# Hybrid HGRN2 and MoBA layer: the first pair of MoBA's keys and queries by 512-column products with both parts of x^T

## The chip, the cores and the metric

The kernel runs on one core of a Trainium2 chip, in one launch. The metric is the device time of an execution in microseconds. Before the change the median of three executions is 497.51 us (497.19 to 497.54).

## The reference

The layer reads x (256 tokens by 1024 channels, fp32) and computes

- `proj = x @ w_in`, split into HGRN2's q, f, i, g (1024 columns each), MoBA's q, k, v (1024 each) and 2048 gate logits;
- HGRN2, a gated linear recurrence with 8 heads of 128, then an RMS norm per head, multiplied by `silu(g)`;
- MoBA, which at 256 tokens and blocks of 256 is plain causal attention, 8 heads of 128, with rotary embedding on q and k:

```
t1, t2 = halves of a head
rope(t) = [t1 * cos - t2 * sin, t2 * cos + t1 * sin]
```

- both branches through their own 1024 by 1024 matrix, mixed by sigmoid gates, through `w_out`, added to `2**0.25 * x`, a layer norm;
- a SwiGLU FFN of width 2816, again with a residual and a layer norm.

## The kernel before, in words

**Two-part products.** Each fp32 operand is kept as a high part (rounded to the format that TensorE streams quickly, float32r) and a low part, the difference. A product is high times high, plus low times high, plus high times low. `split` makes the parts: a copy on ScalarE (ACT) and a subtraction on VectorE (DVE). For weights, `stage` issues the load on SP's queue (L203), the copy (L204) and the subtraction (L206), tile by tile in the order of `plan()`, three tiles ahead of their use; there are three buffers for raw tiles and four each for high and low parts.

**x^T.** `xp` is a `Pair`: for each of the 8 slices of 128 channels, the high and the low part of x^T lie side by side, 256 tokens each. `xTh` and `xTl` are views of one part; `xp.both(k)` is both parts as one operand of 512 columns.

**Two forms of a projection by features** (128 output features on the partitions, 256 tokens along the row; a pair is two such features, which here are two heads):

- `feat_pair` (narrow): one PSUM bank for the two features. For each feature and each k, three matmuls of 256 columns (L303 to L305): high weight by high x, high weight by low x, low weight by high x, all added into the same 256 columns.
- `wide_pair` (wide): one PSUM bank per feature. For each k, one matmul of 512 columns (L293: high weight by both parts of x) and one of 256 (L294: low weight by high x, added to the first half). The sum of the two halves of the bank is made afterwards, by the caller.

MoBA's keys and queries come in four pairs of heads each. `rope_pair` (L613) makes one: the pair j = 0 by `feat_pair`, with the rotary embedding read from PSUM; the others by `wide_pair`, with the halves summed into a tile of the pool `sm`, tag sg (a copy on ACT, L619, and an add on DVE, L620), from which the embedding is read. The embedding is two copies on ACT that swap the halves (L624, L625), a multiplication by cos on DVE (L626), and a multiplication by sin and an addition on POOL (L627, L628). Tag sg has two buffers. They also hold the swapped halves `rt`, and the squares `sq` of HGRN2's norm (L517).

**PSUM.** Pool `mm` has four banks (all projections), pool `aux` the other four (recurrence, heads, transpositions).

**Order.** At the start and from the last part of the mixing to the first of the FFN, and at the end, the order on PE, DVE and ACT is written out by hand (`manual_schedule`). Between these, a planner with its own cost estimates sorts the instructions of each engine before the run; on the chip each engine then works through its list in order and waits by semaphores. The priority comes from the order in the program. There HGRN2 runs as a side task (`side.step()`): around the first key and query pair stand its last products (`sc`, L503, and `o`, L514 and L515), the norm (squares L517 on ACT, sums L519 and L520 on DVE, the power on POOL L521, the product L524 on DVE), the transpositions (`ot`, L533, on PE) and their split (L536, L537). MoBA's heads (scores L632 and L633) follow as a side task after two pairs each.

The order of the projections in the program is: values for the recurrence, its gate, half of MoBA's values, gate b, key pair 0, query pair 0, key pair 1, query pair 1, the other half of the values, pairs 2 and 3, gate a.

Of the kernel before, what the change touches and what calls it, by code (L numbers as in the profile page):

```python
# [10 lines left out]
F32 = mybir.dt.float32  # L11
# [6 lines left out]
P = 128  # L18
T = 256
# [101 lines left out]
def hybrid_layer_kernel(ctx: ExitStack, tc, x, xw, vecs, bias, wts, ln1_w, ln1_b, ln2_w, ln2_b, consts, out):  # L121
    nc = tc.nc
# [6 lines left out]
    sm = pool("sm", 2)  # L129
    klp = pool("klp", 1)  # L130
    mm = pool("mm", 4, space=PSUM)
# [106 lines left out]
    def fetch(ahead=LOOKAHEAD):  # L238
        while state["next"] < len(loads) and len(ready) < 1 + ahead:
            list(stage())  # L240
        return ready.pop(0)
# [6 lines left out]
    xp = Pair("xp")  # L248
# [27 lines left out]
    def feat_pair(name, ah=None, al=None):  # L276
        ah, al = (xTh, xTl) if ah is None else (ah, al)
        wh, wl = fetch()
        ps = mm.tile([P, 2, T], F32, tag="mm", name=name)
        for f in range(2):  # L280
            feat_steps(ps[:, f, :], wh, wl, f, ah, al, range(KC))
        return ps

    def wide_pair(name, a, p, tag):


        wh, wl = fetch()
        pss = []
        for f in range(2):
            ps = p.tile([P, 2, T], F32, tag=tag, name=f"{name}{f}")  # L290
            wcol = slice(f * P, (f + 1) * P)
            for k in range(KC):
                nc.tensor.matmul(ps, wh[:, k, wcol], a.both(k), start=(k == 0), stop=False)  # L293
                nc.tensor.matmul(ps[:, 0, :], wl[:, k, wcol], a[0, k, slice(0, T)],  # L294
                                 start=False, stop=(k == KC - 1))
            pss.append(ps)
        return pss

    def feat_steps(ps, wh, wl, f, ah, al, ks, k0=0):
        wcol = slice(f * P, (f + 1) * P)  # L300
        for k in ks:
            kk = k0 + k
            nc.tensor.matmul(ps, wh[:, k, wcol], ah[:, kk, :], start=(kk == 0), stop=False)  # L303
            nc.tensor.matmul(ps, wh[:, k, wcol], al[:, kk, :], start=False, stop=False)  # L304
            nc.tensor.matmul(ps, wl[:, k, wcol], ah[:, kk, :], start=False, stop=(kk == KC - 1))  # L305
# [99 lines left out]
    for j in range(4):  # L405
        ps = feat_pair(f"hq{j}")
        sg = sm.tile([P, 2, T], F32, tag="sg", name=f"sgq{j}")
# [203 lines left out]
    ybl = slot("ybl", F32R).rearrange("p (h t) -> p h t", h=H)  # L611

    def rope_pair(nm, dst, j):  # L613
        if j == 0:
            ps = feat_pair(f"m{nm}{j}")
        else:
            ps = sm.tile([P, 2, T], F32, tag="sg", name=f"z{nm}{j}")
            for f, parts in enumerate(wide_pair(f"m{nm}{j}", xp, mm, "mm")):
                nc.scalar.copy(ps[:, f, :], parts[:, 1, :])  # L619
                nc.vector.tensor_add(ps[:, f, :], parts[:, 0, :], ps[:, f, :])  # L620
        hs = slice(2 * j, 2 * j + 2)
        bc = lambda z: z[:, None, :].to_broadcast([P, 2, T])
        tmp = sm.tile([P, 2, T], F32, tag="sg", name=f"rt{nm}{j}")
        nc.scalar.copy(tmp[0:64], ps[64:P])  # L624
        nc.scalar.copy(tmp[64:P], ps[0:64])  # L625
        nc.vector.tensor_mul(dst[:, hs, :], ps, bc(cos))  # L626
        nc.gpsimd.tensor_mul(tmp, tmp, bc(sin))  # L627
        nc.gpsimd.tensor_add(dst[:, hs, :], dst[:, hs, :], tmp)  # L628
# [44 lines left out]
    for c in range(2):  # L673
        if c == 1:
            values(1)
        for j in range(2 * c, 2 * c + 2):
            rope_pair("k", kT, j)
            side.step()
            rope_pair("q", qT, j)
            side.step()  # L680
        side.gens.append(moba_heads(4 * c, 4))
# [318 lines left out]
```

## Time and profile before

| | |
|---|---|
| median of three executions | 497.51 us (497.19 to 497.54) |
| profiled execution | 497.34 us |
| its span | 495.5 us |
| mean granted TensorE clock | 0.995 |
| busy: PE, DVE, ACT, POOL | 486.4, 396.9, 279.4, 34.0 us |
| instructions: PE, DVE, ACT, POOL | 2662, 495, 350, 33 |

Times are microseconds from the start of the span. PE is TensorE's matmul, PEld its weight load, which overlaps; DVE is VectorE, ACT is ScalarE, POOL is GpSimd, SP the engine that issues most loads. In the order of time a row has the start, the duration, the engine, the line and what is written from what; names are those of the program without buffer numbers. Matmuls are pipelined: a matmul's duration reaches into the next one's, so that what one costs in a stream is read from the distance between starts. A product of plain fp32 operands shows as two matmuls.

### The profile page before, as it was taken

The numbers are of one execution on the slowest core, as the hardware profiler recorded it, in microseconds if no ns is written. First come the engines' busy times: TensorE is split into PE (matmuls) and PEld (weight loads), VectorE is DVE, ScalarE is ACT, GpSimd is POOL, SyncE is SP. The second block draws the span as 40 slices with busy tenths as digits, with TensorE's granted clock in tenths as the row PEclk, the third lists the DMA queues.
The fourth block names the chain that finished last, engine by engine and source line by source line (L and its number), as shares of the span: only waits on it lengthen the run. The fifth ranks groups of instructions, "written<-read, shape, count | busy, mean of one in ns | idle before, by whom it ended". The sixth has DMA issues, their size and how long they took to land.

```text
span 495.5 us, 6725 instructions
## 1 busy us (share of the span) xinstructions
PE 486.4 (98%) x2662; PEld 422.0 (85%) x2662; DVE 396.9 (80%) x495; ACT 279.4 (56%) x350; POOL 34.0 (7%) x33
## 2 busy tenths in 40 slices
PE   9999999999999999999999999999999999999993
PEld 8899888888899888888888888888888888888883
DVE  4978799999868797876595778854887778899997
ACT  5796487435546676669643462444566554565510
POOL 0000000000003631240000000000000000000001
PEclk9999999999999999999999999999999999999997
DMA  8977526644542437358455446256555454355502
GB/s 310 417 259 285 169 92 248 222 161 169 171 169 89 142 126 285 112 167 306 181 176 175 165 176 242 87 187 237 175 202 219 169 177 165 128 227 221 188 1 85
DMA packets 14703, 92.65 MB, mean 187 GB/s; under 512 B 1744, under 2 KB 1744, under 8 KB 4944
## 3 DMA queue, kind: packets, MB, share of 16 engines
q1 hardware_dynamic: 13824, 89.08, 49.7%
q0 software_dynamic: 848, 3.15, 2.0%
q8 instruction: 21, 0.34, 0.3%
q14 instruction: 10, 0.08, 0.0%
HBM read 91.17 MB, written 1.05 MB: 186 GB/s over the span
## 4 chain that ended last, share of the span: by engine, by line
PE 96%; DVE 2%; DMA 1%; issue 0%; ACT 0%; DVEq 0%
PE fu L293 7%; PE fg L293 7%; PE fg L294 3%; PE fu L294 3%; PE mq L293 2%; PE mk L293 2%; PE sc L483 2%; PE wp L923 2%; PE wp L924 2%; PE wp L922 2%; PE hq L304 2%; PE hq L305 2%; PE hq L303 2%; PE hf L317 2%; PE za L339 1%; PE za L341 1%
## 5 line engine op out<-in xcount | busy, mean ns | idle before, releaser
L206 DVE TENSOR_TENSOR wl<-raw,wh 128x2048 fp32r<-128x2048 f32 (+1 forms) x72 | 164.5, 2291 | 55.1 <-ACT wh L204 54.9
L204 ACT CAST wh<-raw 128x2048 fp32r<-128x2048 f32 (+1 forms) x72 | 135.4, 1888 | 65.7 <-PE fg L293 11.5
L293 PE MATMUL fg<-x1p,wh 128*128 128x512 f32 x144 | 50.5, 394 | 0.0
L293 PE MATMUL fu<-x1p,wh 128*128 128x512 f32 x144 | 50.4, 394 | 0.0
L294 PE MATMUL fg<-x1p,wl 128*128 128x256 f32 x144 | 40.0, 278 | 0.0
L294 PE MATMUL fu<-x1p,wl 128*128 128x256 f32 x144 | 39.9, 277 | 0.0
L293 PEld LDWEIGHTS fu<-x1p,wh 128*128 128x128 f32 x144 | 27.0, 187 | 6.2
L293 PEld LDWEIGHTS fg<-x1p,wh 128*128 128x128 f32 x144 | 27.0, 187 | 6.1
L294 PEld LDWEIGHTS fg<-x1p,wl 128*128 128x128 f32 x144 | 27.1, 188 | 0.1
L294 PEld LDWEIGHTS fu<-x1p,wl 128*128 128x128 f32 x144 | 27.1, 188 | 0.0
L304 PE MATMUL hq<-xp,wh 128*128 128x256 f32 x64 | 18.1, 283 | 0.0
L305 PE MATMUL hq<-xp,wl 128*128 128x256 f32 x64 | 18.1, 283 | 0.0
L303 PE MATMUL hq<-xp,wh 128*128 128x256 f32 x64 | 18.1, 283 | 0.0
L293 PE MATMUL mk<-xp,wh 128*128 128x512 f32 x48 | 17.5, 402 | 0.0
L293 PE MATMUL mq<-xp,wh 128*128 128x512 f32 x48 | 17.2, 399 | 0.0
L485 DVE COPY_PREDICATED SD<-cst,sc 128x512 f32<-128x512 uint32 x14 | 14.9, 1071 | 1.2 <-PE sc L483 1.0
L733 PE MATMUL wp<-wh,ap 128*128 128x512 f32 (+1 forms) x40 | 14.9, 373 | 0.0
L732 PE MATMUL wp<-wl,ap 128*128 128x512 f32 (+1 forms) x40 | 14.9, 373 | 0.0
L731 PE MATMUL wp<-wh,ap 128*128 128x512 f32 (+1 forms) x40 | 14.9, 373 | 0.0
L521 POOL TENSOR_TENSOR ost<-ost,half 128x4 f32<-128x4 f32 x4 | 4.0, 1012 | 154.0 <-DVE ost L520 154.0
L294 PE MATMUL mk<-xp,wl 128*128 128x256 f32 x48 | 13.8, 288 | 0.0
L294 PE MATMUL mq<-xp,wl 128*128 128x256 f32 x48 | 13.6, 284 | 0.0
(319 smaller groups left out, 1319.7 us busy)
## 6 DMA issues: line engine op xcount, KB each, us to landing
raw<-in_wts_dram SPq DMA_DIRECT2D x76, 1024.0 KB, 4.8
xw<-in_xw_dram SPq DMA_DIRECT2D x6, 640.0 KB, 9.6
raw<-in_wts_dram SPq DMA_DIRECT2D x2, 512.0 KB, 10.6
xr<-in_x_dram POOLq DMA_DIRECT2D x1, 1024.0 KB, 5.6
wb<-in_ln_w_dram POOLq DMA_DIRECT2D x2, 512.0 KB, 5.6
wb<-in_ln_b_dram POOLq DMA_DIRECT2D x2, 512.0 KB, 7.5
out_dram<-y SPq DMA_DIRECT2D x4, 256.0 KB, 2.1
cst<-in_consts_dram SPq DMA_DIRECT2D x1, 960.0 KB, 12.2
```

What stands on the lines that cost most here:

```text
L204: nc.scalar.copy(h[:, ks, :], raw[:, ks, :])
L206: eng.tensor_sub(l[:, ks, :], raw[:, ks, :], r32(h[:, ks, :]))
L293: nc.tensor.matmul(ps, wh[:, k, wcol], a.both(k), start=(k == 0), stop=False)
L294: nc.tensor.matmul(ps[:, 0, :], wl[:, k, wcol], a[0, k, slice(0, T)], start=False, stop=(k == KC - 1))
L303: nc.tensor.matmul(ps, wh[:, k, wcol], ah[:, kk, :], start=(kk == 0), stop=False)
L304: nc.tensor.matmul(ps, wh[:, k, wcol], al[:, kk, :], start=False, stop=False)
L305: nc.tensor.matmul(ps, wl[:, k, wcol], ah[:, kk, :], start=False, stop=(kk == KC - 1))
L317: nc.tensor.matmul(ps, wh[:, kk, wcol], xp.both(k), start=False, stop=False)
L485: nc.vector.copy_predicated(later(SD, n, 4 * g, 4), m[:, None, :, :, :].to_broadcast([P, 4, nb, NT, n]), ps.rearrange("p a (b u i) -> p a ...
L731: nc.tensor.matmul(ps, lh(kk)[:, ts], wh[:, k, ns], start=(kk == first), stop=False)
L732: nc.tensor.matmul(ps, lh(kk)[:, ts], wl[:, k, ns], start=False, stop=False)
L733: nc.tensor.matmul(ps, ll(kk)[:, ts], wh[:, k, ns], start=False, stop=(kk == ktot - 1))
```

## The change

Key and query pair 0 take the form of the other three pairs. `feat_pair` is called for HGRN2's q alone then.

```diff
     def rope_pair(nm, dst, j):
-        if j == 0:
-            ps = feat_pair(f"m{nm}{j}")
-        else:
-            ps = sm.tile([P, 2, T], F32, tag="sg", name=f"z{nm}{j}")
-            for f, parts in enumerate(wide_pair(f"m{nm}{j}", xp, mm, "mm")):
-                nc.scalar.copy(ps[:, f, :], parts[:, 1, :])
-                nc.vector.tensor_add(ps[:, f, :], parts[:, 0, :], ps[:, f, :])
+        ps = sm.tile([P, 2, T], F32, tag="sg", name=f"z{nm}{j}")
+        for f, parts in enumerate(wide_pair(f"m{nm}{j}", xp, mm, "mm")):
+            nc.scalar.copy(ps[:, f, :], parts[:, 1, :])
+            nc.vector.tensor_add(ps[:, f, :], parts[:, 0, :], ps[:, f, :])
         hs = slice(2 * j, 2 * j + 2)
```

For each of the two projections this replaces 48 matmuls of 256 columns by 16 of 512 and 16 of 256, takes two banks of `mm` in place of one, adds a tile of tag sg, two copies on ACT and two adds on DVE, and lets L624 to L626 read that tile in SBUF in place of the bank. Loads, weights and their splits stay as they are.

## The prediction

> **What bounds the kernel now.** I read the page first: the busy shares, the forty slices and the chain that ended last.
>
> ```profile
> span 495.5 us, 6725 instructions
> ...
> PE 486.4 (98%) x2662; PEld 422.0 (85%) x2662; DVE 396.9 (80%) x495; ACT 279.4 (56%) x350; POOL 34.0 (7%) x33
> ...
> PEclk9999999999999999999999999999999999999997
> ...
> PE 96%; DVE 2%; DMA 1%; issue 0%; ACT 0%; DVEq 0%
> ```
>
> TensorE is busy for 98% of the span, at full granted clock up to the last of the forty slices, and the chain is 96% PE. What no other engine can hide is PE's own issue time; work on DVE, ACT or POOL counts only where it makes PE wait. Second view: busy times in the stretch where the first key and query pair runs now, and in the next pair's (columns: stretch, length, busy us and instructions of PE, PEld, DVE, ACT and POOL, granted clock, DMA share, GB/s).
>
> ```profile
> 139.60:159.10 19.50, 19.50 (x170) 19.46 (x169) 13.36 (x27) 10.94 (x15) 3.35 (x4) 1.00 0.36 133
> 159.10:171.50 12.40, 12.40 (x75) 10.89 (x75) 10.41 (x17) 7.99 (x12) 7.85 (x5) 1.00 0.32 94
> ```
>
> PE fills both. In the first stretch DVE has 19.50 - 13.36 = 6.1 us free and ACT 8.6 us. Busy PE can hide small gaps, because a matmul's end is modelled, so the third view is the order of time on PE, from which I take start-to-start distances (columns: start, duration, engine, line).
>
> ```profile
> 29.78 0.28 PE L303 MATMUL hq<-xp,wh 128*128 128x256 f32 x1
> ...
> 41.66 0.28 PE L303 MATMUL hq<-xp,wh 128*128 128x256 f32 x1
> ...
> 156.90 0.28 PE L305 MATMUL mq<-xp,wl 128*128 128x256 f32 x1
> ...
> 159.05 0.28 PE L305 MATMUL mq<-xp,wl 128*128 128x256 f32 x1
> 159.17 0.40 PE L293 MATMUL mk<-xp,wh 128*128 128x512 f32 x1
> ...
> 165.69 0.40 PE L293 MATMUL mq<-xp,wh 128*128 128x512 f32 x1
> ...
> 170.98 0.40 PE L293 MATMUL mq<-xp,wh 128*128 128x512 f32 x1
> ...
> 339.76 0.39 PE L293 MATMUL fu<-x1p,wh 128*128 128x512 f32 x1
> ...
> 344.27 0.39 PE L293 MATMUL fu<-x1p,wh 128*128 128x512 f32 x1
> ```
>
> A step over one k is three 256-column matmuls in the narrow form, one 512 and one 256 in the wide form. Narrow: 11.88 us for the 33 steps of hq is 0.360 us a step, 2.15 us for the last 6 of mq is 0.358. Wide: 5.29 us for 15 steps of the second pair's mq is 0.353, 4.51 us for 13 steps of fu is 0.347. Both stream 768 columns; the wide one only has a matmul and a weight load less.
>
> **The change, part by part.**
>
> *TensorE.* Two projections, two features, eight k: 32 steps. 96 matmuls become 64. In place, 32 x (0.358 - 0.353) = 0.16 us less; between the rows farthest apart, 32 x (0.360 - 0.347) = 0.42 us less. No row has a wide step longer than a narrow one, so there is no loss at this term. I take 0.2 us, because the hq run and the second pair's mq, the longest uninterrupted runs of this region, give 32 x (0.360 - 0.353) = 0.22 and the in-place pair a little less. [...]
>
> *The order on PE.* The planner lays the HGRN work between these matmuls and may lay it otherwise. That costs nothing by itself:
>
> ```profile
> 150.59 0.28 PE L303 MATMUL mq<-xp,wh 128*128 128x256 f32 x1
> 150.71 0.27 PE L533 MATMUL ot<-cst,on 128*128 128x128 f32 x1
> 150.74 0.36 PE L304 MATMUL mq<-xp,wh 128*128 128x256 f32 x1
> 150.94 0.28 PE L305 MATMUL mq<-xp,wl 128*128 128x256 f32 x1
> ...
> 151.18 0.27 PE L533 MATMUL ot<-cst,on 128*128 128x128 f32 x1
> ```
>
> L303 to L305 is 0.35 us with a transposition between, against 2 x 0.12 = 0.24 without: the insertion costs 0.11 us. In the chain, four transpositions one behind the other cost the same 0.11 us each:
>
> ```profile
> 165.06 0.44 PE ot L533 x4
> ```
>
> So breaking the stream costs nothing beyond the inserted work; no gain comes from fewer breaks and no loss from more.
>
> *ACT and DVE.* Four copies (L619) and four adds (L620) are new; L624 and L625 now read the sum in SBUF, L626 too.
>
> ```profile
> L619 ACT COPY zk<-mk x6: 357/370/374, 162.6 to 205.7; 128x256 f32<-128x256 f32 x6
> L620 DVE TENSOR_TENSOR zk<-mk,zk x6: 408/414/418, 165.2 to 208.5; 128x256 f32<-128x256 f32 x6
> ...
> L624 ACT COPY rtk<-mk x1: 583/583/583, 157.5 to 157.5; 64x512 f32<-64x512 f32 x1
> ...
> L626 DVE TENSOR_TENSOR kT<-mk,cst x1: 677/677/677, 160.0 to 160.0; 128x512 f32<-128x512 f32 x1
> L624 ACT COPY rtk<-zk x3: 619/619/620, 170.6 to 209.0; 64x512 f32<-64x512 f32 x3
> L626 DVE TENSOR_TENSOR kT<-zk,cst x3: 674/680/683, 171.2 to 209.2; 128x512 f32<-128x512 f32 x3
> ```
>
> ACT: 4 x 0.370 + 4 x (0.619 - 0.583) = 1.6 us. DVE: 4 x 0.414 = 1.7 us, L626 unchanged. Both fit into the 8.6 and 6.1 us that are free under PE's matmuls, so they cost nothing; with that cover gone they would cost at most their 3.3 us in a row. The new waits are those of L619, for its bank's last matmul and a buffer of sg, and of L620 behind it; queued behind them are weight splits on both engines and the norm's squares and sums. What could be late next is thus (a) weights, (b) PSUM banks, (c) the heads that read kT and qT, and the norm, which is the first rival below.
>
> (a) Weight tiles are split long ahead. This cast waited for mk's last use of its buffer, and four buffers turn round, so it holds the tile four products on, after mq, mk and mq: mv's first (mk, mq, mk and mq are one tile each):
>
> ```profile
> 149.95 1.90 ACT L204 CAST wh<-raw 128x2048 fp32r<-128x2048 f32 x1 [1.20 <-PE mk L304]
> 151.94 2.28 DVE L206 TENSOR_TENSOR wl<-raw,wh 128x2048 fp32r<-128x2048 f32 x1
> 171.33 0.40 PE L339 MATMUL mv<-wh,xp 128*128 128x512 f32 x1
> ```
>
> Its low part ends at 154.2, 17 us before PE needs it; 3.3 us more on ACT and DVE don't reach PE. The change adds no DMA and moves none past another on SP's queue; the number of weight tiles is the same.
>
> (b) The four banks of the pool mm now hold this pair's four halves, and the second pair's first product, at 159.17 in today's order, needs the first of them. Rows for mk, a square's last reading, the end of qT's first pair on POOL, and the first scores:
>
> ```profile
> L303 PE MATMUL mk<-xp,wh x16: 277/283/283, 139.7 to 149.5; 128*128 128x256 f32 x16
> ...
> 157.55 0.69 DVE L519 TENSOR_REDUCE ost<-sq 128x4 f32<-128x512 f32 x1 [0.46 <-ACT sq L517]
> ...
> L632 PE MATMUL s<-kT,qT x16: 270/272/275, 174.1 to 244.5; 128*128 128x128 f32 x16
> ...
> 165.89 1.30 POOL L628 TENSOR_TENSOR qT<-qT,rtq 128x512 f32<-128x512 f32 x1
> ```
>
> Even all of mk is done by 149.8, over 9 us ahead; copy and add take 0.8 us. The two buffers of tag sg, into which the sum goes, are shared with the squares of the norm, the last of them read until 158.2. A half that got its buffer only then would be summed at 159.0, still ahead of 159.17. I cost it at zero; otherwise a late bank costs a copy and an add, 0.8 us.
>
> (c) Scores of the first head start at 174.1; qT of the first pair is finished on POOL at 165.89 + 1.30 = 167.2. 7 us are to spare.
>
> **The sum.** Profiled execution: 497.34 us, of which 495.5 are span and 1.84 lie around it. 497.34 - 0.2 = 497.1. That execution lies 0.17 below the median of 497.51, so for a median I forecast 497.51 - 0.2 = 497.3 us.
>
> **The rivals.**
>
> *Slower: PE waits for the HGRN norm's transpositions.* Squares, sum, power on POOL, product on DVE, transposition on PE: a chain whose PE part sits between the matmuls of this pair with next to no slack, in an order fixed before the run.
>
> ```profile
> 150.89 1.13 DVE L524 SCALAR_TENSOR_TENSOR on<-o,ost,hgs 128x128 f32<-128x128 f32 x4 [1.13 <-POOL ost L521]
> ...
> 162.34 2.33 DVE L206 TENSOR_TENSOR wl<-raw,wh 128x2048 fp32r<-128x2048 f32 x1
> ...
> 158.79 1.29 POOL L627 TENSOR_TENSOR rtk<-rtk,cst 128x512 f32<-128x512 f32 x1 [1.50 <-ACT rtk L625]
> 160.25 1.01 POOL L521 TENSOR_TENSOR ost<-ost,half 128x4 f32<-128x4 f32 x1 [0.17 <-DVE ost L520]
> ...
> 162.48 3.34 POOL L627 TENSOR_TENSOR rtq<-rtq,cst 128x512 f32<-128x512 f32 x1
> ```
>
> The transposition at 151.18 starts 0.3 us after the products of its norm began. Behind a rope multiplication on POOL stood a power (160.25), and such a multiplication took 3.34 us in place of 1.29 while a weight split ran. Should the change move the pair's rope so that a held one stands before a power, the products come 3.34 - 1.29 = 2.05 us late, and PE stands with its transposition at its head, all later matmuls behind it: 497.3 + 2.05 = 499.4. It decides once the delay exceeds the planned slack. Against it: PE has no such gap today, although one rope operation was held. Of the first pair's two multiplications by sine, one was held and the other stood before a power; that both meet in the new order, with too little slack, I put at 1 in 10. [...]
>
> *Slower: the banks.* As in (b), with 0.8 us each for both projections' first halves: 497.3 + 1.6 = 498.9. For it: all four banks are now this pair's. Against: 9 us of cover. 4 in 100.
>
> *Faster.* Each wide step at fu's 0.347 gives 0.42 us: 497.1. Over 0.2% (1.0 us, what a measurement of this kernel can tell from no change) needs more than PE's streams hold, as interruptions cost nothing. 3 in 100, for something at the ends of the run that these rows don't show.
>
> **How the numbers follow.** Forecast without visible change 83 in 100, transposition wait 10, banks 4, faster 3. Slower by over 0.2% is thus 0.13 (the banks' case is only just beyond the bound, so I count part of it as same), faster 0.03, same 0.84. Low end: 497.51 - 0.42, less 0.35 for the spread of the three runs, is 496.7. High end: 497.3 + 0.8 for one late bank or a held port, plus part of the 2.05 us wait, 498.9.
>
> **What would show it.** Right: mk and mq of the first pair as L293 x64 and L294 x64 each, no L303 for them, steps of 0.353 us; PE busy throughout to the same end; L619 and L620 x8 for each. Wrong: a PE start-to-start distance of over 0.5 us between 139 and 175 us, with ot or o (POOL's power late) or mk (bank late) behind it; a PE span more than 0.5 us shorter would show that I missed a cost of the narrow form.

## The result, and the profile after

After the change the median is 502.1 us (501.57 to 502.9, five executions), before it in the same rounds 497.19 us (496.81 to 497.54). The ratio is 1.0096, its 95% interval 1.0086 to 1.0107: slower by 4.9 us, where 497.3 was forecast and 498.9 was the end of the range. The profiled execution took 502.9 us, the longest of the five.

From the page of the kernel after: span and instructions, busy times, the forty slices of PE and of the granted clock, the chain, and the group of mk's 512-column products, all four pairs (busy time, mean ns, idle time ahead of them and its releaser).

```profile
span 501.1 us, 6671 instructions
...
PE 488.3 (97%) x2630; PEld 421.7 (84%) x2630; DVE 398.5 (80%) x499; ACT 280.3 (56%) x354; POOL 32.3 (6%) x33
...
PE   9999999999997999999999999999999999999993
...
PEclk9999999999999899999999999999999999999997
...
PE 93%; DVE 4%; DMA 1%; POOL 0%; issue 0%; ACT 0%; DVEq 0%; POOLq 0%
...
L293 PE MATMUL mk<-xp,wh 128*128 128x512 f32 x64 | 25.7, 434 | 3.4 <-DVE zk L617 3.4
```

TensorE has 32 matmuls fewer, as the change says, and is busy 1.9 us longer all the same (488.3 against 486.4). Of the rows of slices two show a dent: PE in the thirteenth, the granted clock in the fourteenth (a slice is 12.5 us). The chain has 4% of DVE where it had 2%. The last row has the place: PE stood 3.4 us in front of a product of tile mk until DVE's add at L617. (L617 is L620 of the kernel before; from the diff on, lines are three lower: L616 is the copy of the sum, L621 and L622 the swapping copies, L623 the product by cos.) No other row of the view of waits has PE waiting between 139 and 175 us.

The order of time on PE in the kernel after (start, duration, engine, line, operation, and in brackets the idle time and its releaser), around that place:

```profile
149.48 0.39 PE L293 MATMUL mq<-xp,wh 128*128 128x512 f32 x1
...
152.25 0.40 PE L293 MATMUL mq<-xp,wh 128*128 128x512 f32 x1
...
158.37 0.39 PE L515 MATMUL o<-hv,SD 128*128 128x128 f32 x2
158.59 0.27 PE L533 MATMUL ot<-cst,on 128*128 128x128 f32 x1
162.23 0.79 PE L293 MATMUL mk<-xp,wh 128*128 128x512 f32 x1 [3.36 <-DVE zk L617]
...
163.03 0.63 PE L293 MATMUL mk<-xp,wh 128*128 128x512 f32 x1
...
167.51 0.51 PE L293 MATMUL mk<-xp,wh 128*128 128x512 f32 x1
```

The first two rows are pair 0's queries in the new form: eight steps in 2.77 us, 0.346 each. Then two things go wrong. The transposition at 158.59 needs 0.12 us and the next matmul starts at 162.23: **3.52 us stand still**. And the steps that follow take (167.51 - 163.03) / 7 = 0.640 us in place of 0.353: **half speed**. Busy times of short stretches of the same kernel say from when to when (columns as in the prediction; the granted clock is the number after POOL's):

```profile
160.60:160.80 0.20, 0.00 (x0) 0.00 (x0) 0.20 (x2) 0.00 (x0) 0.00 (x0) 1.00 0.00 0
160.80:161.00 0.20, 0.00 (x0) 0.00 (x0) 0.20 (x2) 0.11 (x1) 0.00 (x0) 0.82 0.00 0
161.00:161.20 0.20, 0.00 (x0) 0.00 (x0) 0.20 (x2) 0.20 (x1) 0.00 (x0) 0.50 0.00 0
...
167.20:167.60 0.40, 0.40 (x3) 0.30 (x3) 0.40 (x1) 0.14 (x1) 0.23 (x1) 0.50 0.00 0
167.60:168.00 0.40, 0.40 (x4) 0.36 (x4) 0.38 (x1) 0.40 (x1) 0.00 (x0) 0.81 0.00 0
```

A mean of 0.82 between a clock of 1 and one of 0.5 puts the fall at 160.93, the 0.81 of the last row the return at 167.75. From 162.23 on that is 5.52 us of work at 0.640 a step instead of 0.353: 5.52 x (1 - 0.353 / 0.640) = 2.48 us lost.

On PE, pair 0's own products got cheaper. Adding up, in the order of time, each matmul's distance to the next instruction on PE, mk and mq of pair 0 took 5.90 + 6.16 = 12.06 us before and 5.79 + 5.72 = 11.51 after: 0.55 less. (An instruction inserted between them lengthens such a distance, a transposition by 0.11 us, so that this is not the form alone; the part on TensorE below takes it apart.) The balance is 3.52 + 2.48 - 0.55 = 5.45 us; the spans differ by 501.1 - 495.5 = 5.6.

Why was the bank so late? ACT and DVE in the kernel after, in the order of time (L536 and L537 split the transpositions, L206 splits weights):

```profile
158.04 0.83 ACT L536 ACTIVATE yah<-ot,vec 128x256 fp32r<-128x256 f32 x2
158.79 0.60 ACT L517 ACTIVATE sq<-o 128x512 f32<-128x512 f32 x1
159.29 0.64 ACT L616 COPY zk<-mk 128x256 f32<-128x256 f32 x2
```

```profile
158.17 2.29 DVE L206 TENSOR_TENSOR wl<-raw,wh 128x2048 fp32r<-128x2048 f32 x1
160.38 0.87 DVE L537 SCALAR_TENSOR_TENSOR yal<-ot,vec,yah 128x256 fp32r<-128x256 f32 x2
161.16 0.68 DVE L519 TENSOR_REDUCE ost<-sq 128x4 f32<-128x512 f32 x1
161.76 0.75 DVE L617 TENSOR_TENSOR zk<-mk,zk 128x256 f32<-128x256 f32 x2
```

The first half of mk was complete by 143 us. Its copy ran at 159.29, directly behind the fourth and last square of the norm; its add at 161.76, behind a weight split, two split products and that square's reduction. The 3.52 us are thus: 0.58 from PE's being free (158.71) to the copy, 0.32 for the copy of one half, 2.15 until DVE reaches the add (161.76), and 0.47 for the add and the matmul's start.

The theory to be tested has three parts. (1) The sum comes late because its tile takes its turn in tag sg behind the squares, and so its copy a place behind them in ACT's list. (2) The fourth square reads products o that PE issues immediately ahead of the matmul that needs the bank (158.37), so that the wait is built in, and DVE's queue lengthens it. (3) The half speed is a consequence of the standstill. Rivals: tag sg has too few buffers; the wide form with four banks is slower anywhere; the half speed would have come without the wait.

### The profile page after: what moved, and what is told of

Same layout as the page of the kernel before. It is cut to its first block, busy times and chain, and to the rows that moved or that the text cites. A ratio compares the mean times of both kernels' runs of the same rounds, so it can differ in the third digit from the quotient of the medians.

```text
span 501.1 us, 6671 instructions
## 1 busy us (share of the span) xinstructions
PE 488.3 (97%) x2630; PEld 421.7 (84%) x2630; DVE 398.5 (80%) x499; ACT 280.3 (56%) x354; POOL 32.3 (6%) x33
## 4 chain that ended last, share of the span: by engine, by line
PE 93%; DVE 4%; DMA 1%; POOL 0%; issue 0%; ACT 0%; DVEq 0%; POOLq 0%
PE fu L293 7%; PE fg L293 7%; PE mk L293 3%; PE fg L294 3%; PE fu L294 3%; PE mq L293 2%; PE sc L483 2%; PE wp L919 2%; PE wp L920 2%; PE wp L921 2%; PE mk L294 2%; PE hq L304 2%; PE hq L305 2%; PE hq L303 2%; PE hf L317 1%; PE za L339 1%
## 5 line engine op out<-in xcount | busy, mean ns | idle before, releaser
L206 DVE TENSOR_TENSOR wl<-raw,wh 128x2048 fp32r<-128x2048 f32 (+1 forms) x72 | 164.5, 2290 | 55.5 <-ACT wh L204 55.1
L293 PE MATMUL mk<-xp,wh 128*128 128x512 f32 x64 | 25.7, 434 | 3.4 <-DVE zk L617 3.4
L293 PE MATMUL mq<-xp,wh 128*128 128x512 f32 x64 | 23.1, 401 | 0.0
L294 PE MATMUL mk<-xp,wl 128*128 128x256 f32 x64 | 19.5, 304 | 0.0
L293 PEld LDWEIGHTS mk<-xp,wh 128*128 128x128 f32 x64 | 13.3, 207 | 6.6 <-DVE zk L617 3.6
L294 PE MATMUL mq<-xp,wl 128*128 128x256 f32 x64 | 18.1, 283 | 0.0
```

Source lines behind the costliest of these rows:

```text
L206: eng.tensor_sub(l[:, ks, :], raw[:, ks, :], r32(h[:, ks, :]))
```

## The experiments

Diffs are against the kernel after unless another is named; "before" is always the kernel before, in the same rounds.

**The sum in its own buffer.** The edit touches nothing else; run twice, the profile is from the second.

```diff
-        ps = sm.tile([P, 2, T], F32, tag="sg", name=f"z{nm}{j}")
+        ps = (cp if j == 0 else sm).tile([P, 2, T], F32, tag="z" if j == 0 else "sg", name=f"z{nm}{j}")
```

> As changed, but the summed halves of pair 0 go into a buffer of their own (pool cp, one buffer that the key's and the query's sum share) instead of tag sg. Theory A (the sums wait for the norm's squares, which are ahead of them in tag sg, so the banks of mm come free late and PE stands 3.5 us, then runs at half clock): the first sum is made soon after its product, PE has no wait over 0.3 us before the second pair, granted clock full, 497.0 us (496.6 to 497.6). Rival B (the wait comes from the new order of the recurrence's work on PE, whatever buffer the sums use): the wait of some 3.5 us stays, 501 to 502.5 us.

> The kernel with a buffer of its own for the sums of pair 0 once more, for its profile. Theory A: no PE wait between the last o product and mk of the second pair, granted clock 1.0 throughout, the first copy into the sum some 2 us after mk's first half and before the norm's squares, 16 steps of mk at 0.353 us; time 497.0 us (496.6 to 497.6), 0.2 us below the kernel before.

Measured: 497.27 us, ratio 0.9998 (0.9989 to 1.0007), and again 497.19 us, 0.9997 (0.9987 to 1.0007). The loss is gone. ACT and DVE in its order of time:

```profile
142.81 0.37 ACT L616 COPY zk<-mk 128x256 f32<-128x256 f32 x1 [0.59 <-PE mk L294]
150.47 0.36 ACT L616 COPY zk<-mk 128x256 f32<-128x256 f32 x1
```

```profile
143.93 0.42 DVE L617 TENSOR_TENSOR zk<-mk,zk 128x256 f32<-128x256 f32 x1
152.94 0.41 DVE L617 TENSOR_TENSOR zk<-mk,zk 128x256 f32<-128x256 f32 x1
```

The copy now starts as soon as PE has finished the half, 16.5 us earlier than in the kernel after, with the same matmuls, copies and adds. PE's list was laid out anew as well: six steps of the second pair's mk, from 156.56, now stand ahead of the last products o. So this run alone doesn't hold the order on PE fixed; the next one and the one on DVE's queue do, as PE's order around the wait is in both that of the kernel after. Four banks and the wide form are not slow by themselves.

**Three buffers for tag sg.** `bufs=3` on every tile of tag sg (one of five such lines).

```diff
-        ps = sm.tile([P, 2, T], F32, tag="sg", name=f"z{nm}{j}")
+        ps = sm.tile([P, 2, T], F32, tag="sg", bufs=3, name=f"z{nm}{j}")
```

> As changed, with three buffers in tag sg instead of two. If the two buffers are too few (capacity), the third lets the first sum be made by some 153 us and the time is 497.0 us (496.6 to 497.8). If it is the turn that counts (a tile of the tag is granted only after those ahead of it in the program, here the fourth square, which is itself late), the first sum stays behind that square and the time stays 501 to 502.5 us.

Measured: 502.46 us, ratio 1.0111 (1.0093 to 1.013). PE and ACT in its order of time, and short stretches (granted clock after POOL's column):

```profile
158.94 0.27 PE L533 MATMUL ot<-cst,on 128*128 128x128 f32 x1
162.57 0.50 PE L293 MATMUL mk<-xp,wh 128*128 128x512 f32 x1 [3.36 <-DVE zk L617]
```

```profile
159.14 0.60 ACT L517 ACTIVATE sq<-o 128x512 f32<-128x512 f32 x1
159.64 0.64 ACT L616 COPY zk<-mk 128x256 f32<-128x256 f32 x2
```

```profile
163.20:163.40 0.20, 0.20 (x2) 0.14 (x2) 0.20 (x2) 0.20 (x1) 0.00 (x0) 0.55 1.26 532
163.40:166.00 2.60, 2.60 (x10) 2.21 (x9) 2.34 (x8) 2.01 (x6) 2.15 (x2) 0.50 0.55 230
...
166.60:166.80 0.20, 0.20 (x3) 0.20 (x2) 0.20 (x1) 0.00 (x1) 0.20 (x1) 0.91 0.00 0
```

A third buffer changes nothing: the copy still stands directly behind the fourth square. It is the place in the order, not the number of buffers. (That the planner gives out the buffers of a tag in the order of the program would explain it; that was not tried by itself.) Here the clock fell only after the wait, at 163.22, and came back at 166.64: 3.42 us, 1.53 us lost by the same working. 3.51 + 1.53 - 0.55 = 4.5 us, against spans of 500.3 - 495.5 = 4.8.

**The squares out of the turn.** The sum stays in tag sg, the squares get a buffer of their own.

```diff
-                sq = sm.tile([P, 4, P], F32, tag="sg", name=f"sq{g}{u}")
+                sq = cp.tile([P, 4, P], F32, tag="sq", name=f"sq{g}{u}")
```

> As changed, but the four squares of the norm are taken out of tag sg (a buffer of their own that the four share); the sums of pair 0 stay in tag sg with its two buffers. Theory A: it is the squares that are ahead of the sum; with them gone the first copy comes right after mk's first half, no PE wait over 0.5 us, full clock, 497.0 us (496.6 to 497.8). If the tag's other users (the swapped halves) block the sum as well, a wait stays: 498 to 502 us.

Measured: 496.89 us, ratio 0.9987 (0.9976 to 0.9997). The stretch that held the wait:

```profile
158.00:163.00 5.00, 5.00 (x38) 4.67 (x38) 5.00 (x9) 3.12 (x8) 0.92 (x1) 1.00 0.19 39
```

PE is busy throughout, at full clock. (As with the sum in its own buffer, six steps of the second pair's mk stand ahead of the last products o.) With the first and the second experiment this fixes part (1): whoever leaves the common turn, sum or squares, the wait is gone; more room in the same turn does not help.

**DVE's queue.** ACT copies both halves of each of pair 0's banks out, the one that DVE read from PSUM into a buffer of its own; DVE adds from SBUF. The sum stays behind the squares.

```diff
+        if j == 0:
+            low = cp.tile([P, 2, T], F32, tag="z", name=f"y{nm}{j}")
...
+                nc.scalar.copy(low[:, f, :], parts[:, 0, :])
+                nc.vector.tensor_add(ps[:, f, :], low[:, f, :], ps[:, f, :])
```

> As changed, but both halves of pair 0's banks are copied to SBUF by ACT (the second into a buffer of its own) and DVE adds from SBUF, so the bank is free without DVE. The copies still stand behind the fourth square on ACT, as in the changed kernel (159.3 us there). If DVE's queue (a weight split of 2.3 us, a product and a sum of squares ahead of the add) made up some 2 us of the wait, the bank is free at 160.1, PE stands about 1.5 us instead of 3.5, the clock stays full, and the time is 497.0 + 1.5 = 498.5 us (498.0 to 499.0). If the copy's own wait makes up nearly all, it stays near 501 to 502 us.

Measured: 498.16 us, ratio 1.0015 (1.0005 to 1.0026). PE and ACT in its order of time (L618 is the copy of the second half of a bank, L620 the new one of the first):

```profile
158.46 0.27 PE L533 MATMUL ot<-cst,on 128*128 128x128 f32 x1
159.85 0.50 PE L293 MATMUL mk<-xp,wh 128*128 128x512 f32 x1 [1.12 <-ACT yk L620]
```

```profile
158.66 0.60 ACT L517 ACTIVATE sq<-o 128x512 f32<-128x512 f32 x1
159.15 0.37 ACT L618 COPY zk<-mk 128x256 f32<-128x256 f32 x1
```

Without DVE the wait is 159.85 - 158.46 - 0.12 = 1.27 us: the square and two copies, which remain as long as the order stands. Taking DVE out of the bank's release saved 3.52 - 1.27 = 2.25 us, although ACT has one copy more to make first. PE's order is that of the kernel after. That is part (2). The half speed is gone too: the granted clock is 1.00 from 158 to 167 us.

**Work in the gap.** Eleven products of 512 columns that nothing reads, into a bank of `aux`, ahead of key pair 0 in the program; in PE's order they stand directly before the wait.

```diff
+        if nm == "k" and j == 0:
+            fill = aux.tile([P, 2, T], F32, tag="aux", name="fill")
+            for i in range(11):
+                nc.tensor.matmul(fill, ones, xp.both(i % KC), start=(i == 0), stop=(i == 10))
```

> As changed, with 11 matmuls of 512 columns more, whose result nothing reads, in a bank of aux, ahead of pair 0 in the program; they land where PE stood, after the last o product. They fill 11 x 0.228 = 2.5 us of the 3.5 us wait. If the half clock after the wait comes from PE having stood idle for 3.5 us, it is gone: 16 matmuls of mk take 2.8 instead of 5.1 us, and the time is 502.1 - 2.3 = 499.8 us (499.3 to 500.3), the wait for the bank ending where it did. If the half rate has another cause (the bank, or the weights), it stays and the time is 502.1 us or more.

Measured: 500.15 us, ratio 1.0055 (1.0041 to 1.0069). PE in its order of time (L617 is the added work, L621 the add), and the stretch after the wait:

```profile
158.49 2.81 PE L617 MATMUL fill<-xp,ones 128*128 128x512 f32 x11
161.35 0.33 PE L533 MATMUL ot<-cst,on 128*128 128x128 f32 x1
162.20 0.50 PE L293 MATMUL mk<-xp,wh 128*128 128x512 f32 x1 [0.52 <-DVE zk L621]
```

```profile
161.50:167.00 5.50, 4.98 (x29) 4.21 (x29) 4.97 (x14) 2.12 (x5) 3.44 (x3) 1.00 0.46 183
```

The bank is as late as before (162.20), but PE does useless work instead of standing, and the clock stays at 1.00. So much work added makes the kernel 2 us faster than without it (500.15 against 502.1). That is part (3): the half speed comes from the standstill and is worth about 2 us by itself.

**One half of the change at a time.** First the keys alone in the wide form, as in the diff, which is against the kernel before, then the queries alone (the same with `nm == "k"`).

```diff
     def rope_pair(nm, dst, j):
-        if j == 0:
+        if j == 0 and nm == "q":
             ps = feat_pair(f"m{nm}{j}")
         else:
```

> Only the key pair 0 in the wide form, the query pair 0 narrow as before: pair 0 holds three banks of mm, not four, so PE can do the first half of the second pair's key (8 steps, 2.8 us) before it needs a bank that waits for a sum. Theory A: the wait shrinks from 3.5 to some 0.7 us and lies before mk's second half, too short for the clock to fall, so 497.2 - 0.1 + 0.7 = 497.8 us (497.2 to 498.6). Rival B (new order, whatever the banks): a wait of a few us stays, 499 to 502 us.

> Only the query half of the first pair in the wide form, the key half as before: three banks instead of four. The fourth bank takes the second pair's first half, and the next one needed, at about 161.7 us, is that of the narrow key product, which is read last by the DVE product that ended at 160.7 in the kernel before. The theory of the shared turn and the banks: no wait or up to 0.3 us, 497.2 to 497.6, against 498.0 for the mirror image with the key half wide, where that bank waits for a copy and an add behind the fourth square. If instead each wide half costs the same whatever bank comes next, this is 498.0 as well.

Measured: keys alone 498.0 us, ratio 1.0014 (1.0004 to 1.0023); queries alone 497.14 us, 0.9997 (0.9988 to 1.0007). Three banks are taken instead of four, and what counts is which one comes next. With the keys wide, PE in the order of time (L620 is the add):

```profile
161.61 0.28 PE L294 MATMUL mk<-xp,wl 128*128 128x256 f32 x1
162.82 0.50 PE L293 MATMUL mk<-xp,wh 128*128 128x512 f32 x1 [0.93 <-DVE zk L620]
```

With the queries wide, the next one is the narrow key product's. Its last reader, in DVE's order of time:

```profile
159.23 0.69 DVE L626 TENSOR_TENSOR kT<-mk,cst 128x512 f32<-128x512 f32 x1
```

In the first the second pair's first half takes the fourth bank and its second half waits 161.61 + 0.12 to 162.82, 1.1 us, for the sum behind the fourth square. In the second the bank is free at 159.92 and needed at 162.00, where mk's second half starts. In these two a wide half costs what its bank's release costs; it shows no price of its own.

**The same form elsewhere.** The sum of pair 0 in its own buffer as in the first experiment, and HGRN2's four q pairs wide as well (the diff), their sums in tag sg.

```diff
-        ps = feat_pair(f"hq{j}")
+        ps = sm.tile([P, 2, T], F32, tag="sg", name=f"zhq{j}")
+        for f, parts in enumerate(wide_pair(f"hq{j}", xp, mm, "mm")):
+            nc.scalar.copy(ps[:, f, :], parts[:, 1, :])
+            nc.vector.tensor_add(ps[:, f, :], parts[:, 0, :], ps[:, f, :])
```

> A buffer of its own for the sums of pair 0, and the four HGRN q pairs in the wide form too (their sums in tag sg). If the wide form is worth 0.005 to 0.013 us a step and nothing waits, 32 + 64 steps give 0.5 to 1.2 us: 496.5 us (496.0 to 496.9), the fastest of all. If the sums of the q pairs (2 copies and 2 adds a pair, 3 us on ACT and 3.3 us on DVE in all) hold the banks up in a stretch where DVE is over 80% busy, PE waits there and the time is over 497.5 us.

Measured: 504.54 us, ratio 1.0149 (1.0124 to 1.0175). PE and DVE in its order of time, and short stretches:

```profile
45.07 0.28 PE L294 MATMUL hq<-xp,wl 128*128 128x256 f32 x1
49.97 0.77 PE L293 MATMUL hq<-xp,wh 128*128 128x512 f32 x1 [4.62 <-DVE zhq L409]
```

```profile
47.20 2.29 DVE L206 TENSOR_TENSOR wl<-raw,wh 128x2048 fp32r<-128x2048 f32 x1 [1.58 <-ACT wh L204]
49.41 0.75 DVE L409 TENSOR_TENSOR zhq<-hq,zhq 128x256 f32<-128x256 f32 x2
```

```profile
47.60:48.00 0.40, 0.00 (x0) 0.00 (x0) 0.40 (x1) 0.11 (x1) 0.00 (x0) 0.52 0.94 389
...
54.40:54.80 0.40, 0.40 (x4) 0.36 (x3) 0.16 (x1) 0.00 (x0) 0.00 (x0) 0.95 0.00 0
```

There the sum waits for no square, but for a weight cast and its split, and the result is the same: 4.8 us of standstill, then half speed until 54.44. So a sum need not stand behind a square to do this.

**Which part of the fastest version gains?** The kernel before with only the squares moved, and beside it, once more, the kernel after with the squares moved.

> The kernel before with one edit: the norm's squares get a buffer of their own and leave the turn that they share with sums and rope temporaries. It tells apart two readings of the fastest version so far (496.9, wide form and squares moved). If the wide form of the first pair is what gains there, this kernel stays at the kernel before, 497.3, because in it the late rope copy at 157.5 made nothing wait; own_sq_b beside it is then 0.3 to 0.4 us faster. If moving the squares is what gains, this kernel is itself at 496.9 or 497.0 and the wide form is worth nothing by time.

> The changed kernel with the squares in their own buffer, once more beside the kernel before with the same edit, in more rounds: 496.9, 0.4 us under the kernel before, if the earlier difference was real; 497.2, as the version with the sums in their own buffer, if it was spread. TensorE's saving alone makes 0.2 us.

Measured: 497.22 us, ratio 0.9999 (0.9989 to 1.0009), and 496.97 us, 0.9993 (0.9983 to 1.0003). Moving the squares alone is worth nothing that can be seen; the wide form then lies 0.25 us below it. The changed kernel with the squares moved was 0.4 and 0.3 us faster than before; one interval lies just below 1 and the other just reaches it, so that a gain of this size is likely but hardly established.

## Why the prediction was wrong

**TensorE** (0.2 us less, bounds 0.16 and 0.42): right in sign, a little small. Uninterrupted, pair 0's queries take 0.346 us a step and its keys 0.351 (eight steps from 139.40 to 142.21), not the 0.353 taken from the second pair's mq; 16 x (0.360 - 0.346) + 16 x (0.360 - 0.351) = 0.37, inside the bounds and near the far one. The rest of the 0.55 us of pair 0 is put down to the work that the two kernels insert between its matmuls, of which such distances contain a part.

**The order on PE** (costs nothing by itself): the insertions do cost 0.11 us each as said. But the new order asked for the bank at 158.71 instead of 159.17, which the prediction had kept as the due time.

**ACT and DVE** (3.3 us, hidden): busy for 1.6 us more on DVE (1.7 forecast) and 0.9 on ACT (1.6 forecast), from the two pages. Where the sum is not behind the squares the work is hidden: with either edit PE does not wait for a bank. **(a)** Weights: no wait on them came up. **(c)** Heads: in the kernel after none waited; with the sum in its own buffer PE waited 0.4 us for qT, in another order, which may be why that version shows no gain (497.2) where the one with the squares moved lies at 496.9. **The transpositions** as a rival: no wait. The held port that the high end of the range counts is shown by no run: in the kernel after, POOL's eight multiplications by sine took 1.28 to 1.39 us each, and between 139 and 175 us PE waited for nothing but the bank.

**(b) The banks: here it failed.** "Even all of mk is done by 149.8, over 9 us ahead; copy and add take 0.8 us", and for a half that gets its buffer late, "summed at 159.0, still ahead of 159.17. I cost it at zero". The right mechanism was on the page and even among the rivals, at 4 in 100 and 1.6 us. Three things were wrong in it.

- *The turn was taken from the old order.* The prediction quoted the swapping copy L624 at 157.5, on a product done by 149.8. That row already shows an instruction that runs 7.7 us late. The kernel before with only the squares moved shows how much of this was the turn; there the same copy stands behind a weight cast and not behind the fourth square, 5.7 us earlier (the row below the list). The delay cost nothing then, when pair 0 held two of the four banks. With four banks held, such a delay falls on PE. And the square that holds it reads products which PE makes immediately before it asks for the bank, so that the 9 us of cover could never count: the fourth square began 0.08 us after PE was free, at 158.79.
- *Copy and add were priced as if both engines stood ready.* They take 0.8 us; with the square ahead of the copy on ACT and the 2.15 us until DVE reached the add, the wait was 3.52 us.
- *The price of standing had no term.* 2.48 us in the profiled execution, 1.53 in that with three buffers.

```profile
151.81 0.58 ACT L624 COPY rtk<-mk 64x512 f32<-64x512 f32 x1
```

## What to carry to other kernels

When a change makes a product hold more PSUM banks until another engine has summed it, follow the sum: which buffer it takes and who is ahead of it in that buffer's turn, what stands before it in each engine's list, and whether PE itself makes the input of one of these just before it needs the bank; an early end of the product says nothing. A buffer that is shared by unrelated work ties their orders together, and a further buffer in the same turn need not untie them; a buffer of its own did. A long standstill of PE has to be priced with the time at half clock that can follow: after 3.5 to 4.8 us it cost 1.5 to 2.5 us more here, after up to 1.27 us nothing; no standstill between was measured.

## What the hardware showed that was not expected

The half speed was in no term of the prediction. Its length is much the same in three kernels, worked out as above: 163.22 to 166.64 with three buffers, 3.42 us; 160.93 to 167.75 in the kernel after, 6.82 us; 47.62 to 54.44 with HGRN2's q wide, 6.82 us. That is once and twice 3.41 us. It began at different times against the wait: 2.07 us after the last matmul's end (158.86) in the kernel after, 2.27 us (45.35) with HGRN2's q wide, and with three buffers only 0.65 us after PE had begun to work again. After waits of 1.27 us (the run on DVE's queue), 1.1 (keys alone) and 0.7 (work in the gap) the clock stayed at 1.00.

The granted clock falls once more near the end of these three executions, when PE has run out of work (its last matmul starts at 492.59 in the kernel after). The falls in the kernel after, with three buffers and with HGRN2's q wide:

```profile
495.40:495.60 0.20, 0.00 (x0) 0.00 (x0) 0.20 (x1) 0.00 (x0) 0.20 (x1) 0.58 0.00 0
...
494.20:494.40 0.20, 0.00 (x0) 0.00 (x0) 0.17 (x2) 0.00 (x0) 0.00 (x0) 0.79 0.93 358
...
498.00:498.20 0.20, 0.00 (x0) 0.00 (x0) 0.20 (x2) 0.00 (x0) 0.00 (x0) 0.94 0.00 0
```

By the same working these falls lie at 495.43, 494.32 and 498.18. From the first fall to this one are 334.50, 331.10 and 450.56 us. Divided by the nearest whole numbers of 3.41 us, 98, 97 and 132, these give 3.4133, 3.4134 and 3.4133 us: in each of the three executions the falls and the return lie whole numbers of one length apart, the one that the half speed lasted once or twice.

In the 3.41 us ahead of the first fall PE was without matmuls for 2.07 us in the kernel after, 2.27 with HGRN2's q wide and 2.76 with three buffers. With three buffers, where the half speed lasted one such length, PE was at work again before the fall; where it lasted two, part of the wait came behind the fall, 1.30 us in the kernel after (160.93 to 162.23) and 2.35 with HGRN2's q wide (47.62 to 49.97). Whether the place of the wait decides between one and two was not tried by itself. It could explain the spread of the changed kernel (501.57 to 502.9), which was not shown. Nor does any run show what sets the length, or how long PE has to stand for a fall.
